# Softmax over rows on one core: late loads as two tiles instead of four, first load issued from SyncE

## The chip, the cores and the metric

One core of a Trainium2 chip. The metric is device time in microseconds (us) of one execution; each quoted time is a median over several runs. A run's span in the profile is about 1.8 us shorter than its time.

The program has no matmuls. ScalarE (ACT) computes exponentials and issues loads, VectorE (DVE) does maxima, reciprocals and scalings, SyncE (SP) issues stores, and the 16 DMA engines move the data.

## The reference

```python
x = np.random.randn(16, 1024, 512).astype(np.float32)      # 33.55 MB
x_scaled = x / 2.0
exp_x = np.exp(x_scaled - np.max(x_scaled, axis=-1, keepdims=True))
out = exp_x / np.sum(exp_x, axis=-1, keepdims=True)        # 33.55 MB
```

There are 16,384 rows of 512 numbers. Each of the 128 partitions takes 128 of them: below, "a row" is one row in every partition, 2 KB per partition and 0.26 MB in all.

## The kernel before

The work is cut into tiles of some rows. `PLAN` gives for each tile its chunks (units of compute) and the place in an arena of 100 rows; a tile whose place is taken by an earlier one is "late" and its load waits for the earlier tile's store.

```python
PLAN = [
    ([3], 0), ([4, 3], 3), ([5] * 3, 10), ([5] * 3, 25), ([5] * 3, 40), ([5] * 3, 55),
    ([5] * 3, 70), ([5] * 3, 85), ([5] * 3, 10), ([4, 3], 3), ([3], 0), ([3], 25),
]
AFTER = {8: 4, 9: 4, 10: 4, 11: 6}   # late tile 8 is loaded after tile 4's exponentials, ...
LAG = 2
SPREAD = 1                           # the second load: its last row over 126 and 2 partitions
...
# DVE: the maximum of chunk k, then reciprocal and scaling of chunk k - LAG
for k in range(len(chunks) + LAG):
    if k < len(chunks):
        do_max(k)          # waits until the whole tile has been loaded
    if k >= LAG:
        do_mul(k - LAG)    # waits for ScalarE's exponentials
...
# SyncE: one store per tile, when its last chunk is scaled
for t in range(len(tiles)):
    nc.sync.wait_ge(s_mul, last_chunk[t] + 1)
    nc.sync.dma_start(out=dram(of, t), in_=sb(t)).then_inc(...)

for t in awaited:                    # GpSimd at the end
    nc.gpsimd.wait_ge(st[t], 16)
nc.gpsimd.wait_ge(s_end, 16 * (len(tiles) - len(awaited)))
```

All loads go out from ScalarE's queue, all stores from SyncE's, so there is one queue of loads and one of stores. The last four tiles have 15, 7, 3 and 3 rows, and DVE works strictly in order.

## Time and profile before

| | before |
|---|---|
| time, median (lowest to highest) | 161.98 us (161.88 to 162.05) |
| span | 160.3 us |
| DVE / ACT busy | 82% / 59% |
| load packets and store packets, share of 16 engines' span | 49.5% + 48.7% |
| moved | 67.14 MB |
| last load lands, DVE's wait for it | 145.7 us, 7.37 us |
| last store issued | 151.7 us |

To read it, ask which resource cannot be given less to do. DVE's 82% and the two queues' 98.2% compete. The page's chain of waits, followed back from the last instruction:

```profile
DVE 78%; DMA 10%; another core or an unknown queue 5%; issue 0%; DVEq 0%
```

The stores that are still in flight afterwards are not instructions and aren't in it.

### The profile page before, as it was taken

How to read it: one execution, taken by the hardware profiler on the slowest of the kernel's cores; microseconds unless marked ns; L12 is line 12 of the kernel's file. 1: busy time of each engine (PE TensorE's matmuls, PEld its weight loads, DVE VectorE, ACT ScalarE, POOL GpSimd, SP SyncE). 2: the span in 40 equal slices, each digit the busy share in tenths (PEclk: the TensorE clock that was granted, in tenths of full speed). 3: DMA queues.
4: the chain of work that ended last, by engine and by line, in shares of the span. 5: the costliest groups of instructions: out<-in, count | busy, mean ns of one | idle time of the engine just before them, and what ended most of it. 6: DMA issues, size and time to landing. Idle time of an engine off the chain costs nothing.

```text
span 160.3 us, 482 instructions
## 1 busy us (share of the span) xinstructions
DVE 131.9 (82%) x155; ACT 94.5 (59%) x257; POOL 0.2 (0%) x4
## 2 busy tenths in 40 slices
DVE  0466499999999999999999999999999999506800
ACT  0639176768448647766688666797666875501300
POOL 0000000000000000000000000000000000000000
DMA  7999999999998989899999999898999999999994
GB/s 279 422 421 391 416 432 431 436 473 382 417 475 383 475 383 483 383 483 424 429 452 406 468 399 468 385 475 376 454 432 452 440 420 425 386 463 445 406 403 179
DMA packets 3603, 67.14 MB, mean 419 GB/s; under 512 B 400, under 2 KB 400, under 8 KB 1296
## 3 DMA queue, kind: packets, MB, share of 16 engines
q10 hardware_dynamic: 1872, 33.56, 49.5%
q1 hardware_dynamic: 1728, 33.56, 48.7%
q14 instruction: 3, 0.02, 0.0%
HBM read 33.55 MB, written 33.55 MB: 419 GB/s over the span
## 4 chain that ended last, share of the span: by engine, by line
DVE 78%; DMA 10%; another core or an unknown queue 5%; issue 0%; DVEq 0%
DVE negmax L100 40%; DVE arena L120 23%; DVE arena L113 13%; DMA arena<-in_x_dram 10%; DVE recip L109 2%; DVEq L215 0%
## 5 line engine op out<-in xcount | busy, mean ns | idle before, releaser
L139 ACT ACTIVATE arena<-arena,negmax 128x512 f32<-128x512 f32 x128 | 90.7, 710 | 49.8 <-DVE negmax L100 49.8
L100 DVE TENSOR_REDUCE negmax<-arena 128x5 f32<-128x2560 f32 (+2 forms) x28 | 72.3, 2585 | 18.8 <-DMA arena<-in_x_dram 18.8
L120 DVE TENSOR_SCALAR arena<-arena,recip 128x512 f32<-128x512 f32 x91 | 37.8, 482 | 0.7
L139 ACT ACTIVATION_READ_ACCUMULATOR arena<-arena,negmax 128x1 f32 x128 | 23.9, 187 | 0.0
L113 DVE TENSOR_TENSOR arena<-arena,recip 128x2560 f32<-128x2560 f32 (+2 forms) x8 | 21.0, 2625 | 0.3
L109 DVE RECIPROCAL recip<-sums 128x5 f32<-128x5 f32 (+2 forms) x28 | 4.9, 176 | 0.0
L139 ACT ACT_TABLE_LOAD x1 | 1.3, 1283 | 5.4 <-issue 5.4
L204 POOL MEMSET const-bfloat16-1.0<- 128x1 bf16 x1 | 0.1, 101 | 0.0
L204 POOL MEMSET const-uint8-127<- 128x1 uint8 x1 | 0.1, 101 | 0.0
L204 POOL MEMSET const-float32-0.0<- 128x1 f32 x1 | 0.1, 98 | 0.2 <-issue 0.2
L204 POOL MEMSET const-float32-1.0<- 128x1 f32 x1 | 0.1, 98 | 0.0
## 6 DMA issues: line engine op xcount, KB each, us to landing
arena<-in_x_dram ACTq DMA_DIRECT2D x7, 3840.0 KB, 42.6
out_dram<-arena SPq DMA_DIRECT2D x7, 3840.0 KB, 23.7
out_dram<-arena SPq DMA_DIRECT2D x2, 1792.0 KB, 12.2
arena<-in_x_dram ACTq DMA_DIRECT2D x3, 768.0 KB, 51.1
out_dram<-arena SPq DMA_DIRECT2D x3, 768.0 KB, 7.6
arena<-in_x_dram ACTq DMA_DIRECT2D x1, 1792.0 KB, 55.6
arena<-in_x_dram ACTq DMA_DIRECT2D x1, 1536.0 KB
arena<-in_x_dram ACTq DMA_DIRECT2D x1, 252.0 KB
```

The lines of the kernel that those rows point to most:

```text
L100: nc.vector.reduce_max(out=negmax[:, b : b + c], in_=arena[:, a : a + c], axis=mybir.AxisListType.X, negate=True,)._wait_ge(ld[t], 48 if t ...
L109: nc.vector.reciprocal(out=recip[:, b : b + c], in_=sums[:, b : b + c])._wait_ge(s_exp, k + 1).then_inc(s_rec, 1)
L113: nc.vector.tensor_mul(out=arena[:, a : a + c], in0=arena[:, a : a + c], in1=recip[:, b : b + c].unsqueeze(2).to_broadcast([P, c, D]),)._w ...
L120: ins = nc.vector.tensor_scalar_mul(out=arena[:, a + r], in0=arena[:, a + r], scalar1=recip[:, b + r : b + r + 1],)
L139: ins = nc.scalar.activation(out=arena[:, a + r], in_=arena[:, a + r], func=mybir.ActivationFunctionType.Exp, bias=negmax[:, b + r : b + r ...
L204: nc = _bacc.Bacc("TRN2", target_bir_lowering=False, num_devices=1)
```

## The change

The intent: fewer and larger late tiles, so that fewer packets (below, the profile's unit of a transfer: one partition's contiguous run) and semaphores (counters by which a DMA reports that it is done) are handled and the last load arrives sooner; the first load from another engine, so that ScalarE can issue the second at once; waits without use removed. The cut of the second load's last row over 126 and 2 partitions stands in both kernels.

```diff
 PLAN = [
     ([3], 0), ([4, 3], 3), ([5] * 3, 10), ([5] * 3, 25), ([5] * 3, 40), ([5] * 3, 55),
-    ([5] * 3, 70), ([5] * 3, 85), ([5] * 3, 10), ([4, 3], 3), ([3], 0), ([3], 25),
+    ([5] * 3, 70), ([5] * 3, 85), ([5] * 3, 0), ([5, 4, 4], 15),
 ]
-AFTER = {8: 4, 9: 4, 10: 4, 11: 6}
+AFTER = {8: 4, 9: 6}
...
+            if t == 0:
+                nc.sync.dma_start(out=sb(t), in_=dram(xf, t)).then_inc(ld[t], 16)
+            elif t == SPREAD:
...
-        for t in awaited:
-            nc.gpsimd.wait_ge(st[t], 16)
         nc.gpsimd.wait_ge(s_end, 16 * (len(tiles) - len(awaited)))
```

More of the change, by code (lines that the diff above doesn't have):

```diff
@@ L87, in issue_loads @@
         for t in range(begin, end):
-            if t == SPREAD:
+            if t in behind:
+                continue
+            if t == 0:
+                nc.sync.dma_start(out=sb(t), in_=dram(xf, t)).then_inc(ld[t], 16)
+            elif t == SPREAD:
                 r = tiles[t][1] - 1
@@ L94, in issue_loads @@
                     ).then_inc(ld[t], 16)
-            elif t not in behind:
+            else:
                 nc.scalar.dma_start(out=sb(t), in_=dram(xf, t)).then_inc(ld[t], 16)
```

## The prediction

> **What bounds the kernel now.** The kernel reads 33.55 MB and writes 33.55 MB once each, so I read first the line of DMA activity in the page (share of 40 slices, GB/s), then the waits, then the end.
>
> ```profile
> DVE 131.9 (82%) x155; ACT 94.5 (59%) x257; POOL 0.2 (0%) x4
> DMA  7999999999998989899999999898999999999994
> DMA packets 3603, 67.14 MB, mean 419 GB/s; under 512 B 400, under 2 KB 400, under 8 KB 1296
> q10 hardware_dynamic: 1872, 33.56, 49.5%
> q1 hardware_dynamic: 1728, 33.56, 48.7%
> ```
>
> The 16 DMA engines are busy in every slice but the first and the last, and the packets of the load queue (q10) and the store queue (q1) together fill 98.2% of the span. DVE is 82% busy. The chain of waits names DVE for 78% of the span, which misleads: it walks back over an engine that is almost always busy, but DVE could finish early and the bytes would still have to go out. The table by stretches decides it (columns: stretch, length, DVE, ACT and POOL busy, granted clock, DMA share, GB/s):
>
> ```profile
> 20.00:67.00 47.00, 46.69 (x31) 31.11 (x85) 0.00 (x0) 1.00 1.00 429
> 67.00:110.00 43.00, 42.68 (x61) 31.36 (x88) 0.00 (x0) 1.00 1.01 434
> 110.00:134.00 24.00, 23.82 (x38) 18.44 (x53) 0.00 (x0) 1.00 1.01 434
> 134.00:145.50 11.50, 4.07 (x8) 2.84 (x8) 0.00 (x0) 1.00 1.03 442
> 148.00:152.00 4.00, 3.55 (x11) 1.69 (x6) 0.00 (x0) 1.00 0.89 383
> 152.00:158.00 6.00, 0.00 (x0) 0.00 (x0) 0.00 (x0) 1.00 0.97 408
> ```
>
> Between 134 and 145.5 us DVE works 4.07 of 11.5 us, yet the DMA engines are as full as ever: idle time of DVE there costs nothing as long as stores are queued. 67.1 MB at 430 GB/s is 156 us; bytes begin to move at about 1.2 us and end at about 158. That is the whole time. Only from 148 us on do the engines thin out (0.89, then 0.97).
>
> The second thing to see is why DVE idles there. It waits 7.37 us for the last load, of three rows, until 145.68:
>
> ```profile
> 145.68 1.75 DVE L100 TENSOR_REDUCE negmax<-arena 128x3 f32<-128x1536 f32 x1 [7.37 <-DMA arena<-in_x_dram]
> ```
>
> That load was queued at 94.6 us and took 51.1 us. In the stretch from 135 to 145 us the DMA view lists the two queues so (packets, MB, share):
>
> ```profile
> q1 hardware_dynamic: 133, 3.59, 83.4%
> q10 hardware_dynamic: 125, 0.68, 16.2%
> ```
>
> Nearly as many packets each, but 5.3 times the bytes for the stores. A packet here is one partition's contiguous run: 15 rows of 2 KB are 30 KB, three rows 6 KB, and 6/(6+30) is 17%. So a load of few rows beside stores of 15 rows gets a sixth of the bandwidth. From 70 to 90 us, where both sides have 15 rows, the same view gives 4.49 and 4.27 MB, about half each.
>
> **What the Trainium skill says.** The page "DMA: Bandwidth & Descriptors", section "Queues, rings and completion order", says that each DMA engine takes turns between queue rows packet by packet. The trace agrees: 133 packets against 125 while the bytes stand 5.3 to 1. [...] The section "Issuing engines are not separate DMA queues" says that DMAs started by different engines end up on the same 16 DMA engines, so issuing from several saves only issue time. For the first load moved to SyncE I expect just that; the table agrees in so far as the total stays near 430 GB/s whether one queue is busy or both. "Where 436 GB/s comes from" gives 435 GB/s as the ceiling of 16 engines; the 434 of the table is at it, so there is no rate to be won, only idle gaps.
>
> **The change part by part.** The second load's rows over 126 and 2 partitions are in both kernels; the diff only reorders that code.
>
> First load on SyncE. Before, ScalarE issued it at 0.13 us (0.38 us of its queue) and the second load's first part at 0.54. Now both go out at once. The 0.79 MB of the first load then share the engines with the second load: beside its 12 KB packets the first load's 6 KB ones get a third, so it lands after 0.79 + 1.57 MB instead of after 0.79 MB: 2.36 MB at 430 GB/s is 5.5 us against 1.8. I expect its landing near 8 us instead of 4.5. DVE's first reduction slips by over 3 us, but DVE idled 3.08 us before the second load (start 9.38) and 3.55 us before the third (18.27), so the slip is swallowed by 18.27; the first store goes out about 1 us later, while loads fill the engines anyway. Bytes may start up to 0.1 us earlier. Worth to the end: 0 to 0.1 us.
>
> Two late loads instead of four. Both kernels have the same first 100 rows, and the load of rows 86 to 100 (tile 8) was queued at 67.9 and took 42.6 us: it lands at 110.5. Then 13 rows, 3.41 MB, remain. Before they took until 145.65, 35 us. Now they are packets of 26 KB beside 30 KB: 13/28 is 46%, or 200 GB/s, so 17 us: landing near **127.5 us, 18 us earlier**. DVE reaches the first reduction of that tile at 126.3 as before and waits about 1.2 us instead of 7.37. From there by the chain's own durations: reduction of five rows 2.73, scaling of five 2.2 with its reciprocal, reduction of four 2.19, scaling of five 2.2 (store of tile 8 issued near 136.9; before 134.6), reduction of four 2.19, scaling of five 2.2, of four 1.8 and 1.8. Last store issued near **144.9 us**, before 151.7.
>
> This moves nothing by itself. After 127.5 only stores remain: (158 - 127.5) x 0.43 MB/us is 13.1 MB. If tile 8's store enters 1.3 us after issue, at 138.2, 4.6 MB are gone of the 5.8 MB that lay before it: 1.2 MB or 2.8 us in hand. The last store, entering at 146.2, finds 8.0 of 9.7 MB gone: 1.7 MB or 4 us in hand. The store queue doesn't run dry and the end is still bytes over rate.
>
> What does move is small. (a) The thin tail: before, the store of seven rows was held behind the wait at 145.68, was issued at 148.95, and the queue was nearly empty by then. Against 434 GB/s the stretch 148 to 152 lacks 0.20 MB and 152 to 158 lacks 0.16 MB, together 0.8 us if every engine suffers alike; an engine that lagged anyway loses nothing by it. I count 0.3 us. (b) Fewer DMAs: two loads and two stores less, each with eight packets and one semaphore write on each engine. The mean rates by stretch suggest that small packets cost little (408 GB/s where they are 6 KB against 434 with 30 KB); I estimate 0.3 us for 0.8 MB twice in and twice out turned into larger packets. (c) GpSimd's four waits are on stores that landed long before (the fourth tile's before 90 us): 0. **Sum: 0.6 us less, 161.4 us.**
>
> **The rivals.** Rival 1: the earlier end of the loads counts in full, and the tail from the last landing to the end (14.6 us before) moves forward by several us, to 150 to 156 us. For it speaks that DVE's 7.37 us wait is the chain's largest single wait at the end. Against it stands the 442 GB/s during that very wait. It would need a rate above 435.
>
> Rival 2: one store of 13 rows at the end, issued only when all three chunks are scaled, leaves the engines idle: 3.41 MB take 7.9 us and nothing overlaps. Were the last load to land at 135 or later, the store would enter near 153.7 and end at 162 or more, for 165 us. The 46% share speaks against it: 4 us in hand.
>
> Rival 3: the first load's slip of 3 us travels down DVE, which is 99% busy from 20 us on. The wait of 3.55 us before 18.27 speaks against it, since the third load's landing doesn't move. If it did travel, DVE still has 13 us before the end of the bytes, so the time would stay.
>
> **Range and chances.** With the bytes as bound, I see from no gain (161.9) to 1.2 us (160.8), with some noise about it; the measured runs of before spread over 0.17 us. Range 160.7 to 162.1. A change by over 2% is 3.2 us: faster needs rival 1, slower rival 2; 2% and 1%.
>
> **What would show it.** Right: the 13-row load lands between 125 and 130 us; DVE's wait of 7.37 us shrinks below 3; the last DVE work ends near 145 and the last store is issued there; DMA share stays at 0.97 or more from 145 to 157 us; the first reduction starts near 8 us and the third tile's near 18. Wrong: a dip of the DMA share between 136 and 150 us (the queue ran dry), a mean rate in the stores-only stretch well off 430 GB/s, or a third load that lands later than 18.5 us. A lagging engine at the very end could also change by a few tenths for reasons that I can't see in the averages.

## The result, and the profile after

161.69 us (161.59 to 161.76) against 162.01 us (161.88 to 162.08) of the kernel before on the same chip: ratio 0.9981, 95% interval 0.9963 to 0.9998. A ratio here is the mean time of one kernel's fast runs over that of the other's of the same rounds, so not quite the ratio of the medians. The gain is 0.3 us, barely clear of noise, and within 2%.

The page after; the lines answer to those that the prediction shows of the page before:

```profile
span 159.9 us, 476 instructions
DVE 131.6 (82%) x153; ACT 94.4 (59%) x257; POOL 0.2 (0%) x4
DMA  7998999999998989899999999998999998989993
DMA packets 3028, 67.13 MB, mean 420 GB/s; under 512 B 337, under 2 KB 337, under 8 KB 721
q1 hardware_dynamic: 1584, 34.34, 50.1%
q10 hardware_dynamic: 1440, 32.77, 48.1%
```

Nothing that fills the span has changed: the same bytes, the same 98.2% of queues, the same DVE time. Only the packets are fewer, 3,028 for 3,603; the difference of 575 is four DMAs of 128 data packets and 16 small packets for the semaphore each (576), give or take one instruction fetch. Here q1, SyncE's queue, carries the first load as well.

What the change was to move did move. First the table of DVE's work near the end (start, length, engine and line, with its idle time in brackets):

```profile
127.34 2.82 DVE L105 TENSOR_REDUCE negmax<-arena 128x5 f32<-128x2560 f32 x1 [1.06 <-DMA arena<-in_x_dram]
...
143.07 1.68 DVE L125 TENSOR_SCALAR arena<-arena,recip 128x512 f32<-128x512 f32 x4
```

The last load is there at 127.3 instead of 145.7, DVE waits 1.06 us instead of 7.37, and is done at 144.75 instead of 151.6. The DMA view of 110 to 118 us says why (packets, MB, share):

```profile
q1 hardware_dynamic: 60, 1.84, 53.4%
q10 hardware_dynamic: 61, 1.62, 47.0%
```

As many packets on each side, and now nearly as many bytes, since a late load's packet is 26 KB or 30 KB and no longer 6 KB.

And this is what it bought. The stretches after (columns: stretch, length, DVE, ACT and POOL busy, granted clock, DMA share, GB/s):

```profile
20.00:110.00 90.00, 89.37 (x91) 62.51 (x172) 0.00 (x0) 1.00 1.00 431
127.00:145.00 18.00, 17.23 (x31) 10.25 (x29) 0.00 (x0) 1.00 0.99 428
145.00:157.00 12.00, 0.00 (x0) 0.00 (x0) 0.00 (x0) 1.00 1.03 446
```

For the last 15 us no engine computes anything, and the DMA engines are full until 157 us. (A share over 1 is explained with the seven-row store below.) DVE's earlier finish has become a longer wait for the stores: the time that DVE had lost in waiting for the load before, it now spends idle at the end.

The start, in the changed kernel:

```profile
0.00 0.38 SPq L92 DMA_DIRECT2D arena<-in_x_dram  x1
0.12 1.36 ACTq L97 DMA_DIRECT2D arena<-in_x_dram  x3
...
6.71 1.75 DVE L105 TENSOR_REDUCE negmax<-arena 128x3 f32<-128x1536 f32 x1 [6.71 <-DMA arena<-in_x_dram]
...
9.39 3.94 DVE L105 TENSOR_REDUCE negmax<-arena 128x4 f32<-128x2048 f32 x2 [0.93 <-DMA arena<-in_x_dram]
...
14.76 0.34 SPq L166 DMA_DIRECT2D out_dram<-arena  x1
...
18.26 2.82 DVE L105 TENSOR_REDUCE negmax<-arena 128x5 f32<-128x2560 f32 x1 [3.53 <-DMA arena<-in_x_dram]
```

The first load lands 2.2 us later than before (1.7 to 2.2 us in the runs that have the change), because it now shares the engines with the second; by 9.39 us all is as before (9.38), and the first store goes out at 14.76 (14.75 before).

### The profile page after: what moved, and what is told of

Its sections match the earlier page's. It is cut to its first block, busy times and chain, and to the rows that moved or that the text cites. A ratio compares the mean times of both kernels' runs of the same rounds, so it can differ in the third digit from the quotient of the medians.

```text
span 159.9 us, 476 instructions
## 1 busy us (share of the span) xinstructions
DVE 131.6 (82%) x153; ACT 94.4 (59%) x257; POOL 0.2 (0%) x4
## 2 busy tenths in 40 slices
DMA packets 3028, 67.13 MB, mean 420 GB/s; under 512 B 337, under 2 KB 337, under 8 KB 721
## 4 chain that ended last, share of the span: by engine, by line
DVE 58%; DMA 31%; issue 0%; DVEq 0%; ACT 0%
DMA arena<-in_x_dram 31%; DVE negmax L105 30%; DVE arena L125 13%; DVE arena L118 13%; DVE recip L114 1%; DVEq L218 0%; ACT arena L144 0%
## 5 line engine op out<-in xcount | busy, mean ns | idle before, releaser
L105 DVE TENSOR_REDUCE negmax<-arena 128x5 f32<-128x2560 f32 (+2 forms) x27 | 72.1, 2675 | 12.2 <-DMA arena<-in_x_dram 12.2
## 6 DMA issues: line engine op xcount, KB each, us to landing
out_dram<-arena SPq DMA_DIRECT2D x1, 3328.0 KB, 14.2
```

Of the source, the lines that this page charges most:

```text
L105: nc.vector.reduce_max(out=negmax[:, b : b + c], in_=arena[:, a : a + c], axis=mybir.AxisListType.X, negate=True,)._wait_ge(ld[t], 48 if t ...
```

## The experiments

**Theory.** The DMA engines bound the time. The late load's landing and DVE's chain are worth nothing as long as stores are queued ahead of the last one; the 0.3 us come from small things (fewer packets, an earlier first byte, a tail without gaps). **Rivals.** DVE's chain bounds the time and its wait was shortened; or bandwidth is shared by bytes or by DMA, and the earlier landing has another cause; or the last store is about to leave the engines idle.

Twelve kernels ran. Times are medians; "before" is the kernel before in the same rounds.

| run | time us | before us | ratio (95% interval) |
|---|---|---|---|
| first load on SyncE alone | 161.90 | 162.06 | 0.9989 (0.9975 to 1.0003) |
| two late tiles alone | 161.93 | 162.06 | 0.9995 (0.9982 to 1.0007) |
| GpSimd's waits removed alone | 161.97 | 162.06 | 0.9993 (0.9980 to 1.0006) |
| the whole change again | 161.75 | 162.06 | 0.9980 (0.9967 to 0.9992) |
| whole change, second load uncut | 161.45 | 161.99 | 0.9966 (0.9953 to 0.9978) |
| whole change, two rows cut | 162.30 | 161.99 | 1.0020 (1.0006 to 1.0034) |
| before, seven-row store not held | 162.12 | 161.99 | 1.0006 (0.9994 to 1.0019) |
| before, second load uncut | 162.08 | 162.01 | 1.0011 (0.9998 to 1.0025) |
| whole change, late load in pieces | 172.83 | 162.11 | 1.0663 (1.0647 to 1.0679) |
| whole change, one extra reduction | 161.67 | 162.11 | 0.9979 (0.9963 to 0.9995) |
| whole change, four extra reductions | 165.47 | 162.11 | 1.0198 (1.0181 to 1.0215) |
| whole change, fewer scalings | 161.56 | 162.11 | 0.9967 (0.9952 to 0.9982) |

### Does DVE bound the time? 48 scalings taken away

```diff
-        for r in range(c):
+        for r in range(c - 1 if 4 <= t <= 7 else 0, c):
             ins = nc.vector.tensor_scalar_mul(...)
```

The result is wrong: four rows of five in tiles 4 to 7 stay unscaled.

> The changed kernel with only one row in five scaled in tiles 4 to 7 (a wrong result on purpose): 48 of 91 scalings gone, 20 us less DVE work. If the DMA engines bound the time: 161.7, no change, and DVE waits for loads in the middle instead. If DVE bounds it, as the chain of waits suggests: up to 20 us less.

DVE fell to 112.7 us busy. The waits of that run (who waited for whom, us in total, times, longest):

```profile
DVE 112.7 (71%) x105; ACT 93.3 (58%) x257; POOL 0.2 (0%) x4
...
DVE negmax L105 <- DMA arena<-in_x_dram: 30.9, 6, 8.0
```

161.56 us: 19 us of DVE work were worth no more than 0.2 us (the whole change stood at 161.69 and 161.75). The time went into waiting for loads, 30.9 us instead of 12.2. DVE's work before the end is not the bound, whatever its 78% or 58% in the chain of waits; the end of its chain is tested next.

### How much is in hand at the end? One and four extra reductions

```diff
     def do_max(k):
         t, b, c, a = chunks[k]
+        for e in range(EXTRA if k == len(chunks) - 1 else 0):   # 1 or 4
+            nc.vector.reduce_max(out=spare[:, e * c : (e + 1) * c], in_=arena[:, a : a + c],
+                axis=mybir.AxisListType.X, negate=True)._wait_ge(ld[t], 16)
```

> The changed kernel with one extra reduction of four rows (2.2 us of DVE) ahead of the last one. The last store is issued 2.2 us later, near 147. If about 4.4 us of stores are queued ahead of it, nothing changes: 161.7. If DVE's chain at the end bounds the time: 163.9.

> The same with four extra reductions, 8.8 us of DVE. The last store is issued near 153.5. With 4.4 us in hand the queue is empty for about 4.4 us: 166.0 to 166.3. If DVE's chain bounds the time: 170.5; if nothing but bytes counts: 161.7.

One extra reduction: 161.67, no change. Four: 165.47, 3.7 us more than the changed kernel for 8.9 us of delay, and half a microsecond under the range expected. The stretches with four, and the landing of its last store:

```profile
145.00:150.00 5.00, 4.96 (x8) 2.04 (x6) 0.00 (x0) 1.00 0.93 399
150.00:152.00 2.00, 1.97 (x7) 0.89 (x4) 0.00 (x0) 1.00 0.00 0
152.00:154.00 2.00, 1.68 (x5) 0.00 (x0) 0.00 (x0) 1.00 0.00 0
154.00:156.00 2.00, 0.00 (x0) 0.00 (x0) 0.00 (x0) 1.00 1.01 426
...
out_dram<-arena SPq DMA_DIRECT2D x1, 3328.0 KB, 9.3
```

Here is what a dry store queue looks like: DMA share 0.00 for 4 us. A last store that meets an empty queue lands 9.3 us after issue. In the changed kernel it took 14.2:

```profile
out_dram<-arena SPq DMA_DIRECT2D x1, 3328.0 KB, 14.2
```

So 4.9 us of other stores were ahead of it: that is how late DVE may be at no cost. The times say nearly the same: 8.9 us of delay less 3.7 us of loss is 5.2.

### Is bandwidth shared by packet? The late load in pieces

```diff
-                nc.scalar.dma_start(out=sb(u), in_=dram(xf, u)).then_inc(ld[u], 16)
+                for lo, hi in PIECES.get(u, ((0, tiles[u][1]),)):   # {9: ((0,3),(3,6),(6,9),(9,13))}
+                    nc.scalar.dma_start(out=sb(u)[:, lo:hi], in_=dram(xf, u)[:, lo:hi]
+                    ).then_inc(ld[u], 16)
```

Same tile, same bytes, same queue; only the runs per partition are shorter (and the wait is for four times 16).

> The changed kernel with its 13-row late load cut into DMAs of 3, 3, 3 and 4 rows, same tile, same bytes. If queues take turns packet by packet, its packets of 6 KB beside 30 KB get a sixth of the rate: it lands near 142 instead of 127.3 (it would be later but for the store queue running dry), stores are then held up behind it and the time is near 173 to 174 us. If share were by bytes or by DMA, the landing stays at 127 to 128 and the time at 161.7 to 162.

The DMA view of 115 to 130 us in that run, and DVE's reduction that waited:

```profile
q1 hardware_dynamic: 207, 5.38, 83.1%
q10 hardware_dynamic: 206, 1.16, 18.4%
...
142.03 2.82 DVE L107 TENSOR_REDUCE negmax<-arena 128x5 f32<-128x2560 f32 x1 [15.82 <-DMA arena<-in_x_dram]
```

207 packets against 206, but 5.38 MB against 1.16. The load landed at 142.0 (expected 142) and the time was 172.83 (expected 173 to 174). The counts alone would also fit turns by whole DMAs, since the load was cut into four of them; the expectation overlooked that. The start speaks against it: by whole DMAs the first load, which began first, would have landed as early as before, but it landed at 6.7 us, and in the kept trace single 6 KB and 12 KB packets of the two queues alternate from 2.3 us on. Taking turns by packet is shown, and so is what it can cost: the two stores behind that load could not be issued in time, and the DMA share was 0.00 from 148 to 152 us. The kernel before had small late loads at no such price. Its last 13 rows were three separate tiles, of which the second had landed by 134.75 us, so that only the last three rows waited until the end; that this is the reason was not tested.

### Was the thin tail before a loss? The seven-row store not held

```diff
-        for k in range(len(chunks) + LAG): ...
+        ... # as before up to the last maximum, then:
+        do_mul(n - 3)
+        do_mul(n - 2)
+        do_max(n - 1)     # waits for the last load
+        do_mul(n - 1)
```

> The kernel before, with the scalings of the seven-row late tile ahead of the reduction that waits for the last load, so its store is issued near 141 instead of 148.95. The thin stretch of 148 to 152 us (DMA share 0.89) should fill up. If that thin tail cost time at the end: 161.7 or less, the change's gain without its new tiles. If the engine that ends last was never short of work: 162.0.

The store was issued at 139.77 us instead of 148.95, that of the next three rows before 142, and the time did not move. Nor, nearly, did the dip. Stretches of the kernel before, and then of this run:

```profile
148.00:149.00 1.00, 0.96 (x5) 1.00 (x5) 0.00 (x0) 1.00 1.14 492
149.00:150.00 1.00, 1.00 (x3) 0.69 (x2) 0.00 (x0) 1.00 0.59 252
150.00:151.00 1.00, 0.96 (x4) 0.00 (x0) 0.00 (x0) 1.00 0.88 373
```

```profile
148.00:149.00 1.00, 0.00 (x0) 1.00 (x5) 0.00 (x0) 1.00 1.07 461
149.00:150.00 1.00, 0.17 (x1) 0.76 (x3) 0.00 (x0) 1.00 0.67 285
150.00:151.00 1.00, 1.00 (x3) 0.00 (x0) 0.00 (x0) 1.00 0.88 373
```

A store that waits in the queue from 139.77 on cannot be missing at 149. A share of 1.14 cannot be busy time either. The packets in the kept traces, each with its start and duration, settle both. The view books a packet's whole time to the stretch in which it starts: summed in this way, they give its 1.14, 0.59 and 0.88 again. A 30 KB packet takes 1.14 us, and the sizes change from 30 KB to smaller just there. If each stretch gets only the time that lies in it, the engines are 1.00 to 1.01 busy in all three, in this run and in the kernel before, and from 1.00 to 1.04 in every whole microsecond from 3 to 157 us of the kernels before and after (over 1 since packets overlap a little). The dip was neither a shortage of stores nor idle time. This is also the most direct sign of the bound: between 3 and 157 us these sums show no gap to fill.

### The parts alone

```diff
+            if t == 0:                                    # first run: the first load alone
+                nc.sync.dma_start(out=sb(t), in_=dram(xf, t)).then_inc(ld[t], 16)
```

```diff
-... ([5] * 3, 10), ([4, 3], 3), ([3], 0), ([3], 25),     # second run: PLAN and AFTER alone
+... ([5] * 3, 0), ([5, 4, 4], 15),
```

```diff
-        for t in awaited:                                 # third run: these waits alone
-            nc.gpsimd.wait_ge(st[t], 16)
```

The fourth was the changed kernel, unedited.

> The kernel before with the first load alone moved to SyncE. If the time is bytes over a fixed rate plus the moment the bytes start: the first load lands near 6.7 us as in the changed kernel (4.5 before) and the time is 0 to 0.15 us less than before, 161.85 to 162.0. If a later first reduction travelled down DVE, 2 us more. If the whole 0.3 us of the change came from this part: 161.7.

> The kernel before with the late loads as two tiles of 15 and 13 rows alone. If my theory holds, this part carries most of the gain (fewer packets and a tail without gaps): 161.65 to 161.8, last load landing near 127.4, last store issued near 144.8. If the gain came from the other two parts: 162.0.

> The kernel before without GpSimd's four waits for the early stores. They were met long before the end, so 162.0, no change. If they cost something at the end (each wait retired one after the other behind the last), up to 0.2 us less.

> The changed kernel again, beside its parts on the same chip: 161.7, 0.3 us below before. The three parts' gains should add up to this one's.

The ratios of the three parts lie 0.11%, 0.05% and 0.07% below 1, which adds up to 0.23%; the whole measured 0.20%. But each part's interval holds 1.0, so no part is shown to gain anything by itself, and my expectation that the tiles carry most of it (161.65 to 161.8) is not borne out. By the ratios theirs is the smallest of the three, but one run of 162.27 among five makes it so; the order of the three isn't resolved. With the first load alone on SyncE the first reduction began at 6.39 us and nothing later moved by more than 0.2 us: the third tile's began at 18.19 for 18.27.

### The cut of the second load: none, one row, two rows

```diff
-                r = tiles[t][1] - 1
-                for p, q, lo, hi in ((0, P, 0, r), (0, 126, r, r + 1), (126, P, r, r + 1)):
+                for p, q, lo, hi in ((0, P, 0, r + 1),):                      # uncut
```

```diff
-                r = tiles[t][1] - 1
+                r = tiles[t][1] - 2      # two rows over 126 and 2 partitions, in place of one
```

The Trainium skill, page "DMA: Bandwidth & Descriptors", section "Why a DMA increments its semaphore by 16 and not by 1", says that a DMA from ScalarE or SyncE uses the largest number of engines up to 16 that divides its slowest dimension. For 126 that is 14, so the cut spares two engines one row. The packet counts agree: without the cut the page shows 2,884 packets for 3,028, 144 fewer, which is 128 of data and 14 + 2 of semaphores.

> The changed kernel with the second load as one plain DMA over 128 partitions. In the changed kernel the DMA share falls off from about 157.5 us on while the last bytes end near 158.5, so one or two DMA engines finish last. If those are the two engines that the 126-partition DMA spares, they get eight packets of one row back, 0.6 to 0.7 us: the end is that much later, 162.3. If the late engines are others, or no engine is late for good: 161.6 to 161.8.

> The changed kernel with two rows of the second load over 126 and 2 partitions in place of one. If the two spared engines are the late ones, they end about 0.6 us earlier and the others 0.1 us later: 161.1 to 161.3. If the late ones are others: 161.75 to 161.9, a little slower.

> The kernel before with the second load as one plain DMA over 128 partitions. In the changed kernel this took 0.2 to 0.3 us off. If the split costs the same in both kernels (it gives work to engines that end late and spares two that don't): 161.6 to 161.8, as much as the whole change gained. If the split helped the kernel before, whose small late tiles it was tuned with: 162.2 or more.

In the changed kernel the cut hurts: 161.45 without, 162.30 with two rows, both against the same runs of before, 0.85 us apart and well clear of each other. All three times of this group fell outside both of the ranges that I had named for them, and sparing engines more made the end later, not earlier. Uncut, the changed kernel is 0.34% faster than the kernel before, and by the medians 0.2 to 0.3 us faster than the change as made (the two were not run in the same rounds, and their intervals overlap). In the kernel before, taking the cut out gained nothing (1.0011).

The traces show where the loss begins and how the end looks, one profile each. With no row, one and two rows cut, the second tile's first reduction starts at 8.76, 9.39 and 9.99 us, the third's at 17.89, 18.26 and 18.84, and the last load has landed at 127.08, 127.34 and 127.90: the 0.85 us are there from the second load on. The packets by which the last store's 16 engines report their end lie between 157.36 and 158.41 us without the cut. With two rows cut, two engines are done at 157.15 and 157.20, half a microsecond before the next, and the last one at 159.12. So the engines that end last are most likely not the spared ones, which are two (the trace doesn't number the engines). In the kernel before, the start gained as well without the cut (the third tile at 18.01 for 18.27), but the last load did not (145.62 for 145.68). Why the head start lasts in one kernel and not in the other stays open.

## Why the prediction was right

**The bound.** Right, and shown: 19 us less DVE work left the time where it was. The rate with stores alone, for which the prediction's table had only 383 and 408 GB/s, was 428 and 446 after. That the engines thin out from 148 us on was a misreading (see the sum), and rates of 442 and 446 come with shares of 1.03, so they don't speak against the 435 that it took as a ceiling.

**The last load, the wait, the last store.** Landing 127.5 predicted, 127.3 measured (tile 8, on which the reckoning starts, is rows 101 to 115, not 86 to 100; the sums use it rightly); wait 1.2 against 1.06; DVE done and last store issued at 144.9 against 144.75 and 144.8. The share by packets behind it was shown by cutting the load.

**No gain from that.** Right. Rival 1 is dead by the result; rival 2 was closer than its number suggests, since it needs DVE to be only 4.9 us later (predicted: 4 in hand), and with four extra reductions it appeared as drawn.

**The first load.** The mechanism was right, the size off: landing near 8 predicted, 6.7 measured (6.2 to 6.7 over the runs). I had let the two loads share from the first byte to the last; in fact only the first load's packets moved from 1 to 2 us, 34 of them with 0.21 MB. The slip was swallowed before the third tile, as said, and sooner than said: the first store was not even late. Rival 3 did not occur.

**The sum.** 0.6 us less predicted, 0.3 measured. The step that failed is (a), the thin tail, counted at 0.3 us: it was read from shares of 0.89 and 0.97 that turned out to be neither missing stores nor idle time, so it was worth 0. The run with the new tiles alone holds (a) and (b), 0.6 us together by the prediction; it measured 0.08 us (0.05%), with an interval from a gain of 0.3 to a loss of 0.1, and so excludes that sum.

For (b), fewer DMAs, the 0.3 us came from the same shares, by way of the 408 GB/s (taken at its word, 3.1 MB at 408 in place of 434 would be 0.5 us). That its size was about right is luck. The packets of the kept traces give it a better ground: at the median one of 30 KB takes 1,138 ns, of 26 KB 987, of 14 KB 535, of 6 KB 234, which is 37.7 ns per KB and 8 ns for each packet. Four DMAs less are 32 packets, and four semaphore packets of 9 ns, on each engine: 0.29 us, an estimate. In fact the packets' time per engine, the mean of 16, was 157.45 us before, 157.17 with the new tiles alone and 157.07 after. The first load adds a little: its first packet starts at 1.01 us after and 1.15 before. That makes some 0.4 us for the mean engine, of which the time, set by the engine that ends last, shows 0.3. The timed runs are too coarse to share it out, and each of these profiles is a single one. The waits' 0 is within what was measured.

**The signs named.** Confirmed but for one: from 145 to 157 us the share was 1.03; the exception is the first reduction, at 6.7 us and not 8.

## What to carry to other kernels

When the bytes fill the DMA engines, the end is bytes over rate, and a wait of 7 us on a compute engine near the end is free as long as stores are queued: look at the DMA share during the wait before paying for its removal, and measure the slack by adding work there. Queues share the engines packet by packet, so a transfer with short runs per partition beside one with long runs gets the smaller part; give an urgent load runs as long as its rivals'. Don't take dips of a few tenths in one-microsecond stretches for idle time when a single packet lasts as long (1.14 us here).

## What the Trainium skill lacked or had wrong

- "DMA: Bandwidth & Descriptors", section "Queues, rings and completion order": it says that an engine takes turns by packets of some 9 to 17 descriptors, but not that, as these traces count packets, one turn is a partition's whole contiguous run (30 KB here), so that the run length sets a transfer's share: 206 packets carried 1.16 MB beside 207 with 5.38 MB, and the load landed at 142.0 us instead of 127.3.
- The same page, "Issuing engines are not separate DMA queues": it says that DMAs from several engines interleave and that issuing from several only saves issue time, but not that this can delay the earlier of two loads. Moved to SyncE, the first load landed later, with its reduction starting at 6.7 us instead of 4.55, because it then shared the engines with a load that it had preceded on one queue.
- The same page, "Why a DMA increments its semaphore by 16 and not by 1": no page says what it is worth to spare engines in this way. Here two rows over 126 and 2 partitions were 0.85 us slower than none in one kernel, and one row made no measurable difference in another.
